# Attention operands split as whole tiles with their halves placed by DMA, the strict mask as a matmul, and the attentions' GpSimd work on other engines

## The chip, the cores and the metric

The kernel runs on one core of a Trainium2 chip. A core has five engines that run their own instruction streams: TensorE (PE, the matrix engine), VectorE (DVE), ScalarE (ACT), GpSimd (POOL) and SyncE (SP, which here only issues DMAs). They share an on-chip memory (SBUF, 128 partitions) and the matmul accumulators (PSUM, 8 banks of 128 x 512 fp32 words). The metric is the device time of one execution in microseconds (us), lower is better: the median over runs.

## What is computed

Two transformer blocks on 512 tokens of 1024 features, everything in fp32. Block 1 mixes a chunked gated linear attention (GLA) with a multi-head latent attention (MLA, 8 heads, a rotated part of 64 features beside 128 others) and has a feed-forward layer. Block 2 has two attentions of 8 heads of 64 features side by side, then a cross attention over 256 memory rows and a second feed-forward layer. The three attentions that the change touches, cut to their core:

```python
# MLA, one block of queries
s = (einsum('bqhd,bkhd->bhqk', qn_b, k_nope) + einsum('bqhr,bkr->bhqk', qp_b, k_pe)) * scale
p = softmax(where(mask, s, -inf), axis=-1)
o = einsum('bhqk,bkhd->bqhd', p, v)

# forgetting attention ("fox"), c = cumsum(log f) over the tokens
logits = einsum('bhqd,bhkd->bhqk', qi, k) * scale + ci[..., None] - c[:, :, None, :]
p = softmax(where(kpos <= qpos, logits, -inf), axis=-1)
o = einsum('bhqk,bhkd->bhqd', p, v)

# stick-breaking attention ("sb")
z = einsum('bhqd,bhkd->bhqk', qi, k) * scale
strict = kpos < qpos
log_keep = where(strict, log_sigmoid(-z), 0.0)
after = cumsum(log_keep, axis=3, reverse=True) - log_keep
a = where(strict, exp(log_sigmoid(z) + after), 0.0)
o = einsum('bhqk,bhkd->bhqd', a, v)

# block 2 around them
x = x + concat([rmsnorm(fox_o, g1), rmsnorm(sb_o, g2)]) @ w_out
x = x + memory_cross_attention(rmsnorm(x), rmsnorm(mem))
```

## The kernel before

**Numbers as pairs.** The matmuls read operands of the type fp32r; by the kernel's own note each holds 12 significant bits. Every fp32 operand is therefore split into a pair, `hi` (the value cast to fp32r) and `lo` (the value less `hi`): `hi_lo` (L129-142) makes both, `hi` on ScalarE and `lo` on VectorE unless its arguments `eh` and `el` name other engines; `pair` (L148) takes two fresh tiles for it, and `repair` (L380) frees the source as well. A product of two pairs is three matmuls, hi hi, hi lo and lo hi (`mm3`, L205-211). Heads have only 64 features, half of a tile's 128 rows, so the two attentions of block 2 and the rotated part of MLA stack the parts instead: one operand is [hi; lo] over 128 partitions (`stacked`, L1027; in MLA the tiles `Q2`, L756-761), the other a tile [hi; hi] and a tile [lo; lo] (`doubled`, L1035), and two matmuls then do the work.

In `stacked` and `doubled` each half tile of 64 rows is written by an engine of its own: casts on ScalarE and VectorE, differences on GpSimd and VectorE. For the second head of a pair `stacked` writes [lo; hi], with `hi` in the rows where the head's features stand.

**Weights.** `wload` (L175-187) loads a piece of a weight matrix by a DMA on SP's queue into one of three raw buffers (`wr`), then ScalarE casts it (`wh`, L135) and VectorE subtracts (`wl`, L139), 512 columns at a time. While `share_w` is 3 (during MLA only) every third difference goes to GpSimd.

**Order of the work.** The program is written as one Python function that emits products of layers and attention steps interleaved by hand; a scheduler that estimates times then sets the order on each engine. SBUF is cut into 84 slots of 128 x 512 words; `A` takes the slot that was freed longest ago, and whatever fills a slot waits for its last reader. Besides the slots, PSUM banks are taken in rings: for products of layers, for scores, and for sums over keys.

**The stages the change touches.** In MLA (about 325 to 450 us of the profile) `mla_pair` makes the rotated queries and the values of two heads, `mla_qk` the other queries (`qn`) and keys (`kn`), `mla_scores` and `mla_values` go head by head. In fox (950 to 1090 us) `fox_inputs` makes the operands of two heads, a pair, one pair ahead of `fox_scores`; `transposed` and `pv2_step` multiply with the values; `pv2_out` and `close` end a head. In sb (1090 to 1256 us) `sb_inputs` splits the raw queries and keys of a pair. For each of 4 key blocks `sb_keep` works out the logarithm of what the block leaves over: scores z in PSUM, three ScalarE functions into `e`, a maximum and a sum on VectorE (L1072), and the strict mask on the diagonal 128 columns by a product on GpSimd (L1073), then the pair `lkh`, `lkl` on VectorE (L1075, L1076). `sb_values` adds these in PSUM, masks the diagonal by a matmul with `nstrict_r` (L1091), exponentiates and splits the result into `ah` (GpSimd) and `al` (VectorE). Between the sb heads stand other products, from a table: the fox half of the output projection (`half_out`, L1145, its sum into x on GpSimd) and the keys and values of the memory (`memory_keys`, L971, the lower half of its pair on GpSimd). At the seam of fox and sb the norm of the fox output is worked out, with three Newton steps on VectorE (`rsqrt`, L252, on the tile `rtok`).

Of the kernel before, what the change touches and what calls it, by code (L numbers as in the profile page):

```python
# [11 lines left out]
F32R = mybir.dt.float32r  # L12
# [5 lines left out]
P = 128  # L18
# [40 lines left out]
def two_blocks(ctx: ExitStack, tc: tile.TileContext, d, dbg=None):  # L59
# [8 lines left out]
    # ------------------------------------------------------------------ helpers  # L68
    # memory is assigned in the order of the program: a slot is taken from the one freed longest ago
# [37 lines left out]
    def share(**kw):  # L107
        """which banks the products of layers, the scores and the sums over keys take in turn"""
        for name, which in kw.items():
            rings[name] = deque(which)  # L110
# [18 lines left out]
    def hi_lo(hi, lo, src, scale=None, eh=None, el=None):  # L129
        """hi + lo = scale * src, each with 12 significant bits"""  # L130
# [14 lines left out]
    # every how many parts of the weights GpSimd takes one  # L145
# [7 lines left out]
    # the tables of functions are switched here and only here: each switch waits for the functions  # L153
    # before it in the program, and the functions after it wait for the switch
# [20 lines left out]
    def wload(src):  # L175
        """(hi, lo) of each 512 columns of a part of a layer's weights"""
# [4 lines left out]
        for c in range(0, n, T):  # L181
# [3 lines left out]
            # the weights of the layer after a norm wait for the norm  # L185
# [4 lines left out]
    def wtile(w, n, kt, k0=0):  # L190
        """the weights of kt times 128 inputs for the outputs of tile n"""
        step = 8
        ws = []
        for c0 in range(0, kt, step):
            ws.append(wload(w[n, :, (k0 + c0) * P:(k0 + min(kt, c0 + step)) * P]))
        return step, ws

    def wpart(wt, k):
        """(hi, lo) of the 128 columns of input tile k"""
# [12 lines left out]
    def lin(w, n, hs, cols=T, k0=0, after=None):  # L212
        """psum[128 outputs of tile n, cols] = w[:, n].T @ h"""
# [10 lines left out]
    def lin_group(w, ns, hs, wts=None):  # L224
        """as lin for several tiles, the inputs outermost"""
# [9 lines left out]
    def lin_tok(w, b, hs, nt=NT):  # L235
        """psums[token tile][128 tokens, 512 columns of block b]"""
# [13 lines left out]
    def rsqrt(y, src, scale):  # L250
        """1/sqrt(scale * src + EPS) by Newton steps"""
# [11 lines left out]
    class Stat:  # L263
        """sum of squares over features of [features, tokens] tiles, and 1/rms of it; c: the tokens"""
# [26 lines left out]
        def done(self, c=None, direct=False):  # L291
            """1/rms of each token: along the free axis in all partitions, and [token, token tile]"""
# [24 lines left out]
    # ---------------------------------------------------------------- constants  # L317
# [42 lines left out]
    def normed(src_tiles, gain, n, before=None, **kw):  # L360
        """(hi, lo) of gain * x for each tile, and the statistics; the factor 1/rms is put on later"""
# [18 lines left out]
    def repair(x, cols=T, eh=None, el=None):  # L380
        """(hi, lo) of a tile that is freed"""
# [4 lines left out]
    # ---- where one layer ends and the next begins, the tokens go in two halves: the norms of one  # L386
    # ---- half are worked out while the products of the other run
    HALVES = (slice(0, 256), slice(256, 512))

    def last_halves(ns, wts, hs, out, after=None, stat=None, at=(0, 0)):  # L390
        """lin of the last tiles of a layer: all of them for one half of the tokens, then for the other"""
# [18 lines left out]
    def first_halves(at, ns, wts, hs, st, out, before=None, tok=None, tok_out=None):  # L410
        """lin of the first tiles of a layer, for one half of the tokens, then for the other; tok: the
        weights of a product with the tokens outermost that goes along; before: the statistics of the
        norm before; at: the steps that the sums of the norms come before, in either half."""
        for i, c in enumerate(HALVES):
# [27 lines left out]
            else:  # L442
                # the steps of this half: inputs of the product with the tokens outermost, then tiles
# [13 lines left out]
    def chained(src, gain, n, step=None):  # L457
        """(hi, lo) of gain * x for each tile, one half of the tokens after the other, and the statistics"""
# [1047 lines left out]
```

## Time and profile before

| what | value |
|---|---|
| median of 3 runs | 1779.53 us (1779.39 to 1780.85) |
| span of the profiled execution | 1780.0 us |
| PE busy | 1725.7 us, 97% |
| DVE busy | 1150.5 us, 65% |
| ACT busy | 829.5 us, 47% |
| POOL busy | 231.1 us, 13% |

The profile gives the span of the execution that it records and no other time of it. A TensorE busy share of 97% means that nearly all time is matmuls. The shares of the other engines are means over stages that differ: GpSimd does nothing in most stages and a good part of its work in the three attentions. Busy time of the matrix engine isn't all at one speed: a throttle grants it a clock, which the profile gives as a share of the full one.

### The profile page before, as it was taken

How to read it: one execution, taken by the hardware profiler on the slowest of the kernel's cores; microseconds unless marked ns; L12 is line 12 of the kernel's file. 1: busy time of each engine (PE TensorE's matmuls, PEld its weight loads, DVE VectorE, ACT ScalarE, POOL GpSimd, SP SyncE). 2: the span in 40 equal slices, each digit the busy share in tenths (PEclk: the TensorE clock that was granted, in tenths of full speed). 3: DMA queues.
4: the chain of work that ended last, by engine and by line, in shares of the span. 5: the costliest groups of instructions: out<-in, count | busy, mean ns of one | idle time of the engine just before them, and what ended most of it. 6: DMA issues, size and time to landing. Idle time of an engine off the chain costs nothing.

```text
span 1780.0 us, 24148 instructions
## 1 busy us (share of the span) xinstructions
PE 1725.7 (97%) x9007; PEld 1472.4 (83%) x9007; DVE 1150.5 (65%) x2338; ACT 829.5 (47%) x1675; POOL 231.1 (13%) x239
## 2 busy tenths in 40 slices
PE   8999999999998999999999999899999999999997
PEld 6888888888888888888887788787898988888887
DVE  7447863687749542444569667888867587547753
ACT  6534443575534332323426666566525354324442
POOL 0000000343004000000023113563310200000000
PEclk9999999999999999999999999899999999999999
DMA  6212341113531323322501121123404132432221
GB/s 222 82 48 71 93 157 36 48 54 92 181 107 51 116 78 100 109 81 84 165 10 52 54 72 60 40 74 102 136 25 134 57 107 83 131 95 83 73 82 48
DMA packets 51957, 155.30 MB, mean 87 GB/s; under 512 B 5824, under 2 KB 14720, under 8 KB 51840
## 3 DMA queue, kind: packets, MB, share of 16 engines
q1 hardware_dynamic: 51568, 153.55, 28.1%
q8 instruction: 71, 1.16, 0.3%
q14 instruction: 46, 0.38, 0.1%
q10 hardware_dynamic: 144, 0.14, 0.0%
q0 software_dynamic: 128, 0.07, 0.0%
HBM read 151.64 MB, written 2.10 MB: 86 GB/s over the span
## 4 chain that ended last, share of the span: by engine, by line
PE 83%; DVE 11%; ACT 2%; DMA 2%; issue 2%; POOL 1%; SPq 0%; DVEq 0%; ACTq 0%; POOLq 0%
PE bank L207 26%; PE bank L209 26%; PE bank L208 26%; DVE hl L141 2%; DVE wl L139 1%; DVE f L857 1%; DVE dbl L1042 1%; PE bank L734 1%; DMA wr<-w_mk 1%; DVE sq L288 1%; PE bank L300 1%; DVE dbh L1040 1%; DVE lkh L1075 1%; DMA wr<-w_mv 0%; DVE lkl L1076 0%
## 5 line engine op out<-in xcount | busy, mean ns | idle before, releaser
L139 DVE TENSOR_TENSOR wl<-wr,wh 128x512 fp32r<-128x512 f32 (+1 forms) x556 | 377.3, 694 | 289.3 <-ACT wh L135 158.9
L135 ACT CAST wh<-wr 128x512 fp32r<-128x512 f32 (+2 forms) x568 | 333.9, 608 | 458.4 <-PE bank L209 145.5
L207 PE MATMUL bank<-hh,wh 128*128 128x512 f32 (+1 forms) x1380 | 507.3, 369 | 10.2 <-ACT wh L135 7.7
L209 PE MATMUL bank<-hh,wl 128*128 128x512 f32 (+1 forms) x1380 | 506.9, 368 | 1.3 <-DVE wl L139 1.3
L208 PE MATMUL bank<-hl,wh 128*128 128x512 f32 (+1 forms) x1380 | 505.8, 367 | 0.0
L207 PEld LDWEIGHTS bank<-hh,wh 128*128 128x128 f32 x1380 | 261.9, 190 | 51.9 <-ACT wh L135 8.2
L209 PEld LDWEIGHTS bank<-hh,wl 128*128 128x128 f32 x1380 | 262.0, 190 | 44.8 <-DVE wl L139 3.6
L208 PEld LDWEIGHTS bank<-hl,wh 128*128 128x128 f32 x1380 | 262.0, 190 | 40.6 <-DVE hl L141 0.3
L208 PE MATMUL bank<-prl,wh 128*128 128x512 f32 (+1 forms) x471 | 171.4, 364 | 0.0
L209 PE MATMUL bank<-prh,wl 128*128 128x512 f32 (+1 forms) x471 | 171.4, 364 | 0.0
L207 PE MATMUL bank<-prh,wh 128*128 128x512 f32 (+1 forms) x471 | 171.2, 365 | 0.0
L207 PEld LDWEIGHTS bank<-prh,wh 128*128 128x128 f32 x471 | 88.8, 189 | 14.2
L208 PEld LDWEIGHTS bank<-prl,wh 128*128 128x128 f32 x471 | 88.9, 189 | 14.1
L209 PEld LDWEIGHTS bank<-prh,wl 128*128 128x128 f32 x471 | 88.8, 189 | 14.1
L208 PE MATMUL bank<-wl,hh 128*128 128x512 f32 (+1 forms) x192 | 71.9, 377 | 2.2 <-DVE wl L139 2.2
L858 POOL TENSOR_TENSOR x<-x,f 128x256 f32<-128x256 f32 x16 | 13.6, 848 | 459.6 <-ACT hh L137 345.8
L207 PE MATMUL bank<-wh,hh 128*128 128x512 f32 (+1 forms) x192 | 70.3, 378 | 0.1
L209 PE MATMUL bank<-wh,hl 128*128 128x512 f32 (+1 forms) x192 | 70.0, 375 | 0.3 <-DVE hl L141 0.3
L288 POOL TENSOR_TENSOR sq<-sq 128x256 f32<-128x256 f32 x56 | 46.3, 831 | 85.5 <-ACT sq L277 83.1
L137 ACT ACTIVATE hh<-x,vec 128x256 fp32r<-128x256 f32 (+1 forms) x72 | 37.7, 527 | 39.3 <-DVE x L858 16.4
L277 ACT ACTIVATE sq<-x 128x256 f32<-128x256 f32 (+1 forms) x88 | 36.7, 425 | 39.9 <-DVE x L1334 37.8
L139 POOL TENSOR_TENSOR wl<-wr,wh 128x512 fp32r<-128x512 f32 (+2 forms) x12 | 13.2, 1106 | 304.4 <-DVE wl L139 259.4
(389 smaller groups left out, 3000.7 us busy)
## 6 DMA issues: line engine op xcount, KB each, us to landing
wr<-w_fgu SPq DMA_DIRECT2D x44, 512.0 KB, 3.7
wr<-w_up SPq DMA_DIRECT2D x44, 512.0 KB, 3.7
wr<-w1T SPq DMA_DIRECT2D x16, 512.0 KB, 3.8
wr<-w_gate SPq DMA_DIRECT2D x16, 512.0 KB, 3.7
wr<-w_fd SPq DMA_DIRECT2D x16, 512.0 KB, 3.5
wr<-w2T SPq DMA_DIRECT2D x16, 512.0 KB, 3.7
wr<-w_dn SPq DMA_DIRECT2D x16, 512.0 KB, 3.6
wr<-w1K SPq DMA_DIRECT2D x12, 512.0 KB, 4.1
```

What stands on the lines that cost most here:

```text
L135: r = S.copy(hi, src) if eh is S else V.tensor_copy(hi, src)
L137: r = S.activation(hi, src, AF.Copy, scale=scale)
L139: q = el.tensor_tensor(lo, src, f(hi), ALU.subtract)
L141: q = V.scalar_tensor_tensor(lo, src, scale, f(hi), ALU.mult, ALU.subtract)
L207: r = PE.matmul(ps, lhsT=ah, rhs=bh, start=first, stop=False)
L208: PE.matmul(ps, lhsT=ah, rhs=bl, start=False, stop=False)
L209: PE.matmul(ps, lhsT=al, rhs=bh, start=False, stop=last)
L277: S.activation(q[:, :w], src, AF.Square)
L288: self.eadd.tensor_tensor(acc, acc, q[:, :w], ALU.add)
L300: i = PE.matmul(ps[:, 2 * t:2 * t + 2], lhsT=q[:, t * P:(t + 1) * P], rhs=C("ones")[:, 0:2], start=q is acc[0], stop=q is acc[-1])
L734: PE.transpose(tp[:, i * P:(i + 1) * P], ps_tiles[i][:, b * P:(b + 1) * P], C("ident"))
L857: r = V.scalar_tensor_tensor(fs[k][:, c], fs[k][:, c], vcol(gain, k), st.R[:, c], ALU.mult, ALU.mult)
```

## The change

1. *Whole-tile pairs.* The raw tile of two heads (128 rows) is split once, by `repair`: a cast on ScalarE and a difference on VectorE. `stacked` and `doubled` then only copy halves of 64 rows: `place` issues a DMA on SP's queue from one SBUF tile to another. The stacked operand is now [hi; lo] for both heads of a pair. MLA's rotated queries (`Q2`) go the same way. There are 112 such DMAs: 16 in MLA, 48 for fox and 48 for sb.
2. *Strict mask.* In `sb_keep` the product with the mask on GpSimd is gone. One more matmul of 128 columns adds `nstrict_r` (a large negative number where the key isn't strictly before the query) to z in PSUM, as `sb_values` does already. There the softplus of z becomes 0. These are 32 matmuls.
3. *GpSimd left out.* `kn` is cast on ScalarE, and its and `qn`'s differences are on VectorE. `ah` is cast on ScalarE, the lower half of the memory's keys and the sum into x are on VectorE, and `share_w` stays 0, so that VectorE makes all `wl`. In the rotation of MLA one GpSimd product per tile stays.

Outside the three attentions and what stands between their heads, each engine's order is the same. The lines of the changed program lie a little lower: `place` is L754-756, and the former L1072, L1075 and L1076 are L1074, L1076 and L1077.

```diff
...
+    def place(o, rows, src, a):
+        nc.sync.dma_start(f(o[rows]), f(src[a]))
+
+    HALF = (slice(0, 64), slice(64, 128))
+
+    def stacked(p, hh):
+        o = A("stk", F32R)
+        for rows, src in zip(HALF, p):
+            place(o, rows, src, HALF[hh])
+        return o
+
     def mla_pair(hp):
         x = evac(lin(d["w_uq"], 8 + hp, cqs), "qpe", Rq, mscale)
         rope(x)
-        Q2 = [A("Q2a", F32R), A("Q2b", F32R)]
-        S.copy(Q2[0][0:64], x[0:64])
-        G.tensor_tensor(Q2[0][64:128], x[0:64], f(Q2[0][0:64]), ALU.subtract)
-        S.copy(Q2[1][64:128], x[64:128])
-        G.tensor_tensor(Q2[1][0:64], x[64:128], f(Q2[1][64:128]), ALU.subtract)
-        free(x)
+        xp = repair(x)
+        Q2 = [stacked(xp, hh) for hh in range(2)]
+        free(xp)
...
     def mla_qk(hd):
-        qn = repair(evac(lin(d["w_uq"], hd, cqs), "qn", Rq, mscale), el=G)
-        kn = repair(evac(lin(d["w_ukvK"], hd, ckvs), "kn", Rkv), eh=V, el=G)
+        qn = repair(evac(lin(d["w_uq"], hd, cqs), "qn", Rq, mscale))
+        kn = repair(evac(lin(d["w_ukvK"], hd, ckvs), "kn", Rkv))
...
     oms = []
-    share_w[0] = 3
...
     def memory_keys(n, after=None):
-        hi_lo(mk[-1][0][:, cs], mk[-1][1][:, cs], x[:, :NMEM], el=G)
+        hi_lo(mk[-1][0][:, cs], mk[-1][1][:, cs], x[:, :NMEM])
...
-    def stacked(x, hh):
-        o = A("stk", F32R)
-        a, b = (slice(0, 64), slice(64, 128)) if hh == 0 else (slice(64, 128), slice(0, 64))
-        S.copy(o[a], x[a])
-        G.tensor_tensor(o[b], x[a], f(o[a]), ALU.subtract)
-        return o
-
-    def doubled(x, hh):
-        o1, o2 = A("dbh", F32R), A("dbl", F32R)
-        a = slice(64 * hh, 64 * hh + 64)
-        S.copy(o1[0:64], x[a])
-        V.tensor_copy(o1[64:128], x[a])
-        G.tensor_tensor(o2[0:64], x[a], f(o1[a]), ALU.subtract)
-        V.tensor_tensor(o2[64:128], x[a], f(o1[a]), ALU.subtract)
-        return o1, o2
+    def doubled(p, hh):
+        out = []
+        for src in p:
+            o = A("dbl", F32R)
+            for rows in HALF:
+                place(o, rows, src, HALF[hh])
+            out.append(o)
+        return out
...
     def sb_keep(q2, kst, b):
         PE.matmul(z[:, :w], lhsT=kst[:, dg], rhs=q2[0][:, sl], start=True, stop=False)
-        PE.matmul(z[:, :w], lhsT=kst[:, dg], rhs=q2[1][:, sl], start=False, stop=True)
+        PE.matmul(z[:, :w], lhsT=kst[:, dg], rhs=q2[1][:, sl], start=False, stop=False)
+        PE.matmul(z[:, :P], lhsT=ident_r, rhs=nstrict_r, start=False, stop=True)
...
-        G.tensor_tensor(e[:, :P], e[:, :P], C("strict"), ALU.mult)
...
     def sb_values(hd, lks, q2, kst, op, b):
-        hi_lo(ah[:, :w], al[:, :w], a[:, :w], eh=G)
+        hi_lo(ah[:, :w], al[:, :w], a[:, :w])
...
     def fox_inputs(hp):
-        out = [(stacked(xq, hh), doubled(xk, hh)) for hh in range(2)]
-        free(xq, xk)
+        pq, pk = repair(xq), repair(xk)
+        out = [(stacked(pq, hh), doubled(pk, hh)) for hh in range(2)]
+        free(pq, pk)
...
     def sb_inputs(xq, xk):
-        out = [(doubled(xq, hh), stacked(xk, hh)) for hh in range(2)]
-        free(xq, xk)
+        pq, pk = repair(xq), repair(xk)
+        out = [(doubled(pq, hh), stacked(pk, hh)) for hh in range(2)]
+        free(pq, pk)
...
     def half_out(os_, off, Ro, ns):
-            G.tensor_tensor(xs[n], xs[n], y, ALU.add)
+            V.tensor_tensor(xs[n], xs[n], y, ALU.add)
```

**Place 1, VectorE at the start of sb.** The Newton steps of the fox norm (L259 to L261, on `rtok` and the small tiles `sm`) stand among the first head's `e`, `lkh` and `lkl`. Each row is an instruction of VectorE, in its order: line, operation, output<-inputs, partitions x columns. Before:

```order
L261 SCALAR_TENSOR_TENSOR rtok_114<-sm_76,rtok_114 128x4
L1075 TENSOR_SCALAR lkh<-e 128x512
L259 TENSOR_TENSOR sm_76<-rtok_114 128x4
L1076 SCALAR_TENSOR_TENSOR lkl<-e,lkh 128x512
L1075 TENSOR_SCALAR lkh<-e 128x384
L260 TENSOR_TENSOR sm_76<-sm_76,sm_75 128x4
L1040 CAST dbh<-sq 64x512
L1076 SCALAR_TENSOR_TENSOR lkl<-e,lkh 128x384
L261 SCALAR_TENSOR_TENSOR rtok_114<-sm_76,rtok_114 128x4
L1042 TENSOR_TENSOR dbl<-sq,dbh 64x512
```

Of the change, from the same Newton step on (`mk` is the raw key tile of the memory, `mkl` the lower half of its pair):

```order
L261 SCALAR_TENSOR_TENSOR rtok_114<-sm_76,rtok_114 128x4
L139 TENSOR_TENSOR wl<-wr_74,wh 128x512
L1077 SCALAR_TENSOR_TENSOR lkl<-e,lkh 128x512
L259 TENSOR_TENSOR sm_76<-rtok_114 128x4
L375 TENSOR_TENSOR mk<-bank_66,R 128x256
L260 TENSOR_TENSOR sm_76<-sm_76,sm_75 128x4
L139 TENSOR_TENSOR wl<-wr_73,wh 128x512
L261 SCALAR_TENSOR_TENSOR rtok_114<-sm_76,rtok_114 128x4
L1074 SCALAR_TENSOR_TENSOR e<-bank_69,e 128x384
L259 TENSOR_TENSOR sm_76<-rtok_114 128x4
L139 TENSOR_TENSOR mkl<-mk,mkh 128x256
```

The pieces of the next pair's doubled tile (`dbh`, `dbl`) are gone from among the steps, and two lower halves of weights (`wl`) and the memory's keys have come between them.

**Place 2, SP's queue in sb.** The loads of the fox half of the output weights (`w_out2`) and of the memory's weights (`w_mk`, `w_mv`) into the three raw buffers `wr0` to `wr2`. Before:

```order
L179 DMA wr0_72<-w_mk 128x1024
L179 DMA wr2_74<-w_out2 128x512
L179 DMA wr2_74<-w_mk 128x1024
L179 DMA wr0_72<-w_out2 128x512
L179 DMA wr1_73<-w_mk 128x1024
L179 DMA wr0_72<-w_mk 128x1024
L179 DMA wr1_73<-w_mv 128x1024
```

Of the change, where one pair's operands are placed (`prh` and `prl` are the halves of the whole-tile pair, `x2` stands for two copies in a row into the two halves of a tile):

```order
L179 DMA wr1_73<-w_mv 128x1024
L179 DMA wr0_72<-w_mk 128x1024
L756 DMA dbl_10816<-prh_10808 64x512 x2
L756 DMA dbl_10819<-prl_10809 64x512 x2
L756 DMA stk_10822<-prh_10812 64x512
L756 DMA stk_10822<-prl_10813 64x512
L756 DMA dbl_10825<-prh_10808 64x512 x2
L756 DMA dbl_10828<-prl_10809 64x512 x2
L756 DMA stk_10831<-prh_10812 64x512
L756 DMA stk_10831<-prl_10813 64x512
L179 DMA wr2_74<-w_mv 128x1024
```

Twelve copies (four rows stand for two each) now stand in one piece between two loads of weights, and the loads behind them are issued after them.

## Rows read from the trace of the kernel before

**Rows 1.** Page, part 1: busy us, share of the span, instructions of each engine.

```profile
PE 1725.7 (97%) x9007; PEld 1472.4 (83%) x9007; DVE 1150.5 (65%) x2338; ACT 829.5 (47%) x1675; POOL 231.1 (13%) x239
```

**Rows 2.** Busy time by stretch: start:end, us, PE, PEld, DVE, ACT, POOL, PEclk, DMA, GB/s.

```profile
325.00:450.00 125.00, 122.48 (x686) 106.33 (x686) 101.40 (x266) 80.71 (x189) 50.32 (x38) 0.99 0.23 68
600.00:700.00 100.00, 100.00 (x443) 82.82 (x442) 40.69 (x64) 30.66 (x53) 0.00 (x0) 1.00 0.30 90
950.00:1090.00 140.00, 133.92 (x668) 111.12 (x667) 99.14 (x236) 88.34 (x206) 23.91 (x16) 0.98 0.18 55
1090.00:1256.00 166.00, 148.39 (x833) 129.60 (x832) 142.62 (x251) 108.49 (x232) 82.68 (x95) 0.94 0.24 72
```

**Rows 3.** Timeline, PE: start, busy us; in brackets the wait before, its releaser.

```profile
347.21 0.38 PE L208 MATMUL bank<-wl,hh 128*128 128x256 f32 x1 [2.25 <-DVE wl L139]
...
1121.34 1.12 PE L308 MATMUL bank<-con,rtok 128*128 128x128 f32 x4 [3.49 <-DVE rtok L261]
...
1139.74 0.40 PE L207 MATMUL bank<-mh,wh 128*128 128x256 f32 x1 [3.72 <-ACT wh L135]
...
1183.16 0.39 PE L209 MATMUL bank<-mh,wl 128*128 128x256 f32 x1 [3.08 <-DVE wl L139]
```

**Rows 4.** Busy time by stretch, columns as in rows 2: around the last wait.

```profile
1180.00:1190.00 10.00, 6.92 (x32) 6.27 (x32) 9.16 (x14) 4.46 (x12) 9.12 (x11) 0.72 0.19 54
```

**Rows 5.** DVE groups by form, 1088 to 1256 us: count, busy us, mean ns, idle before.

```profile
L139 DVE TENSOR_TENSOR wl<-wr,wh 128x512 fp32r<-128x512 f32 x47 | 36.1, 786 | 5.9 <-ACT wh L135 5.2 <-PE bank L1049 0.7
L1042 DVE TENSOR_TENSOR dbl<-sq,dbh 64x512 fp32r<-64x512 f32 x8 | 8.9, 1113 | 0.2
L1075 DVE TENSOR_SCALAR lkh<-e 128x512 fp32r<-128x512 f32 x8 | 6.9, 860 | 2.2 <-POOL e L1073 2.2
L1076 DVE SCALAR_TENSOR_TENSOR lkl<-e,lkh 128x384 fp32r<-128x384 f32 x8 | 6.5, 815 | 0.1
...
L1072 DVE SCALAR_TENSOR_TENSOR e<-bank,e 128x384 f32<-128x384 f32 x8 | 4.4, 553 | 2.5 <-ACT e L170 2.5
...
L1040 DVE CAST dbh<-sq 64x512 fp32r<-64x512 f32 x8 | 4.4, 545 | 0.2
```

**Rows 6.** The like with GpSimd idle: DVE timeline at 1117, groups 600 to 900 us.

```profile
1117.40 0.43 DVE L1075 TENSOR_SCALAR lkh<-e 128x512 fp32r<-128x512 f32 x1
...
L139 DVE TENSOR_TENSOR wl<-wr,wh 128x512 fp32r<-128x512 f32 x99 | 67.2, 690 | 106.3 <-PE bank L208 52.9 <-ACT wh L135 49.6 <-ACT z L170 1.6
```

**Rows 7.** ACT groups by form, 1088 to 1256 us.

```profile
L135 ACT CAST wh<-wr 128x512 fp32r<-128x512 f32 x49 | 29.7, 618 | 29.4 <-DMA wr<-w_mk 6.0 <-DVE lkl L1076 5.5 <-DVE bol L141 3.5
```

**Rows 8.** POOL groups by form, 1088 to 1256 us.

```profile
L1073 POOL TENSOR_TENSOR e<-e,con 128x128 f32<-128x128 f32 x32 | 18.4, 584 | 21.7 <-DVE e L1072 19.4 <-DVE sm L260 1.9
```

**Rows 9.** Timeline, PE, at 1135 us: two matmuls of 128 columns in a row.

```profile
1135.19 0.28 PE L1091 MATMUL bank<-nstrict_r,ident_r 128*128 128x128 f32 x1
1135.31 0.27 PE L1085 MATMUL bank<-dbh,stk 128*128 128x128 f32 x1
```

**Rows 10.** DVE groups by form, 950 to 1090 us.

```profile
L1042 DVE TENSOR_TENSOR dbl<-fk,dbh 64x512 fp32r<-64x512 f32 x6 | 7.4, 1238 | 0.2
```

**Rows 11.** DVE groups by form, 325 to 450 us.

```profile
L139 DVE TENSOR_TENSOR wl<-wr,wh 128x512 fp32r<-128x512 f32 x14 | 11.6, 839 | 1.4 <-ACT wh L135 0.7 <-PE bank L734 0.4 <-PE bank L208 0.3
...
L135 DVE CAST prh<-kn 128x512 fp32r<-128x512 f32 x8 | 6.1, 767 | 0.1
```

**Rows 12.** Timeline, SP, issuing loads; then DMA issues, us to landing.

```profile
2.15 1.39 SPq L325 DMA_DIRECT2D x<-xT  x3
...
wr<-w2T SPq DMA_DIRECT2D x16, 512.0 KB, 3.7
...
wr<-w_out SPq DMA_DIRECT2D x16, 256.0 KB, 2.8
...
wr<-w_ukvK SPq DMA_DIRECT2D x8, 128.0 KB, 2.0
```

## The prediction, made before the changed kernel was run

> **What bounds the kernel now.** I read the page's busy shares first: TensorE (PE) is busy for 1725.7 of 1780.0 us, GpSimd (POOL) for 231.1 [rows 1]. With PE at 97% the most that a rearrangement can win is what PE waits, 54 us, and what it computes at a lowered clock. So the second view is the busy time by stage [rows 2]: the three attentions that the change touches are MLA (325 to 450 us), the forgetting attention "fox" (950 to 1090) and the stick-breaking attention "sb" (1090 to 1256). PE waits 125 - 122.5 = 2.5 us in the first, 140 - 133.9 = 6.1 in the second and 166 - 148.4 = 17.6 in the third, 26.2 together. The same rows give the granted clock, 0.99, 0.98 and 0.94: (1 - clock) x length is 1.3 + 2.8 + 10.0 = 14.1 us of lost clock. The third view says why: the clock falls after PE has stood still. From 1180 to 1190 us PE waits 3.1 us and the granted clock is 0.72 [rows 3, 4], that is, a part of the stretch ran at the lower of its two levels (1.2 instead of 2.4 GHz). A stall is so paid for almost one and a half times. Together 40 us can be won, and no more.
>
> Who is waited for: the timeline names VectorE (DVE) behind the long waits (the lower half of a weight, `wl`; the Newton steps of a norm, `rtok`) and ScalarE's weight cast `wh` behind one [rows 3]. In sb DVE is busy for 142.6 of 166 us, in the stage 600 to 700, where PE never waits, for 41 of 100 [rows 2]. So the third stage is one where DVE is nearly as full as PE.
>
> A part of DVE's time is no work. In sb the same instruction is long or short: `lkh` of 128x512 takes 860 ns in the mean [rows 5], one that ran with GpSimd idle took 430 [rows 6]; `wl` takes 786 against 690 in the stage without GpSimd; `lkl` of 128x384 takes 815, and `e` of the same size, which reads one operand from PSUM, 553. DVE instructions on SBUF operands stretch where GpSimd works beside them, and GpSimd works for half of the sb stage, 82.7 us [rows 2].
>
> **The change part by part, sb.** *Taken off DVE:* the doubled tiles' differences `dbl` (8.9 us) and casts `dbh` (4.4) [rows 5], 13.3 us. *Put on DVE:* the differences of 8 whole tiles (sq and sk of four pairs, 8 x 0.69 = 5.5), 8 additions to x (8 x 0.69 = 5.5, from `wl`'s unhindered row, also two SBUF operands of 128x512 [rows 6]) and 8 halves of the memory's keys, 128x256 (8 x 0.42 = 3.4, an estimate by 0.69 x 256/512 and the fixed part that 553 against 690 shows), 14.4. *Given back by an idle GpSimd:* 47 x (786 - 690) = 4.5, 8 x (860 - 430) = 3.4, 8 x (815 - 553) = 2.1, so 10.0 from three rows [rows 5, 6]; the 80 other pieces of `lkh`, `lkl` and `al` I take at 0.11 each, a third of what the last two rows give per piece: 9. In sum -13.3 + 14.4 - 19 = -18, DVE goes from 142.6 to about 125 us. ScalarE loses 16 half-tile casts and gets 8 whole ones at the same 0.618 [rows 7] (-4.9) and 32 casts `ah` of 128 to 512 columns, by their mean width 32 x 0.43 = 13.9: from 108.5 to 117.5, still under DVE. The GpSimd step between `e` and `lkh`, 0.58 us each [rows 8], leaves the chain of each key block, and 32 matmuls of 128 columns take its place, 0.12 us from one start to the next [rows 9]: +3.8 us on PE, which is the bound, so they count in full.
>
> What that is worth: PE's own work in sb at full clock is 148.4 - 10.0 + 3.8 = 142 us, DVE's 125, 88% of it; MLA runs today with DVE busy for 101.4 of 125 us, 81%, and PE waits there 2% with the clock at 0.99. Were sb as good, it would take 142/0.97 = 146.5 us, 19.5 less than 166. I take a bit over half, **-11**, because not all of its waits hang on DVE's length: 3.7 us are behind ScalarE's weight cast [rows 3], and ScalarE gets more to do. Bounds: -19.5, and +4 if no wait goes.
>
> *The Newton steps.* The largest single wait that I count on is `rtok`'s 3.49 us at 1121 [rows 3]: between the steps DVE's order held pieces of the next pair's doubled tiles, which are gone there; now a weight's difference and the memory's keys stand between them, but the whole chain begins earlier against PE's matmuls. I count no loss.
>
> **Fox.** DVE loses 8 `dbl` at 1.24 [rows 10] = 9.9 and 8 casts at 0.545 [rows 5] = 4.4, and gets 8 x 0.69 = 5.5: -8.8 of 99.1. The waits to win are 6.1 and 2.8 us of clock, mostly between 968 and 990. Half: **-4.4** (bounds 0 and -8.9).
>
> **MLA.** DVE gets 20 differences of whole tiles (qn, kn, the rotated part: 13.8) and the 12 weight parts that GpSimd took (6 of 0.69, 6 of about 0.5: 7.1), and loses 8 casts of kn at 0.767 = 6.1 and its stretching, 14 x (839 - 690) = 2.1 for `wl` [rows 11] and, by the same ratio for the softmax scaling and the rope sum, some 7: +5 of 101.4, to 87% of PE's time. That cover is thin: **+1**, with bounds -3.8 (all of 2.5 and 1.3 won) and +13 (sb's present share of waits, 10.6%, at nearly the same DVE load).
>
> **The DMAs.** 112 copies of 64 rows x 512 (128 KB): 4 for each of 4 MLA pairs, 12 for each of 4 + 4 pairs later, all on SP's queue, where all weight loads are issued. No copy within SBUF stands in the trace. Issue: three in 1.39 us, 0.46 each [rows 12], so 12 hold the queue for 5.6 us. Landing: 2.0 us by the 128 KB load, 2.8 by the 256 KB one [rows 12]; I take 2.8, since a copy both reads and writes SBUF. A copy waits in the queue for the cast or difference that it copies and for the last reader of the slot that it fills, and the weight loads behind it wait too; who waits for those is ScalarE's `wh`, DVE's `wl` and then PE. The cover of a burst is the weights already split: one tile is 24 matmuls of 0.226 us (443 in the 100 us of the full stage [rows 2]), 5.4 us, about the 5.6 of the burst. Most pairs are copied a head or two ahead, which hides the landing. One is not: the first sb pair, where the lower half of q goes to a slot that the last `fo` step frees; from there 0.5 + 2.8 = 3.3 us stand against 2 us of PE's work, 1.3 exposed. With one more such spot for the weights, **+3**; bounds 0 and the rival below.
>
> Sum against the profiled execution: 1780.0 - 11 - 4.4 + 1 + 3 = 1768.6. The page gives only its span; the runs' median is 1779.53, 0.5 less, so **1768 us**.
>
> **Rivals.** *The queue (slower).* If a copy of 64 rows moves at half the rate of 128 rows, each costs what 256 KB cost: 0.9 us more for each further 256 KB (2.8 to 3.7 [rows 12]), a burst 12 x 0.9 = 10.8 us, 5.4 more than the cover. A wait of that size also draws the lower clock. At one landing and half a slow stretch, 3.7 + 1.7, in half of the eight bursts that is 21.6 us, against 14.4 won: 1779.5 + 7 = **1787**. It decides from 14.4/8 = 1.8 us a burst. For it: 20 copies stand in a row in places, and each sits ahead of the loads. Against: DMA is busy for 18 to 24% of these stages [rows 2]. The Trainium skill says this outright: "DMA: Bandwidth & Descriptors", Rules for kernel authors, advises against two transfers to disjoint halves of the partitions, since they serialize, and for one of 128 partitions; "SBUF — State Buffer", Door 1, has 64 partitions reach 8 of 16 ports. By these the burst would cost the 10.8 us; no row of this trace shows a copy within SBUF.
>
> *Nothing (same).* PE's order is fixed; if the waits are chains and not DVE's load, they form anew a matmul later, and the 3.8 us of PE stay against a few us won: **1779**. For it: `wh` is as often waited for as `wl`. Against: the stretching is measured.
>
> *All of it.* Waits in the three stages sink to what 600 to 700 us shows: 19.5 + 8.9 + 3.8 = 32: **1747**. Against: DVE at 88%.
>
> **How the numbers follow.** Forecast (1758 to 1775) 0.54, everything won 0.12, nothing 0.13, queue 0.21. Faster 0.66, same 0.13, slower 0.21, by the 0.2% (3.6 us) that a measurement of this kernel can tell from no change. The range leaves out the better half of the second case and the upper third of the last: 1750 to 1789.
>
> **What would show it.** Right: in sb `lkh` of 512 columns near 430 ns and `wl` near 690, DVE near 125 us, PE's waits halved and fewer stretches under a clock of 1; 32 more matmuls at L1069. Wrong: PE waiting for `wh` behind a weight DMA that SP issued after a burst; copies landing in over 4 us; new waits in MLA with DVE at 90%.

## The result and the profile after

The changed kernel takes 1769.47 us (median, 1765.36 to 1772.74) against 1779.46 before on the same chip. The ratio is 0.9938, with a 95% interval from 0.9922 to 0.9955. That is 11 us by the ratio and 10 by the medians, inside the range, and 1.5 us above the predicted 1768. The profile of after spans 1767.9 us. That execution's time was 1769.93 us, and in the executions below the time is 1.7 to 2.2 us above the span. The profile of before, 1780.0, so belongs to an execution of about 1782: of the 12.1 us between the two profiles some 2 are scatter.

The page's busy shares after, to be set against [rows 1]:

```profile
PE 1724.3 (98%) x9039; PEld 1472.6 (83%) x9039; DVE 1111.8 (63%) x2366; ACT 832.1 (47%) x1695; POOL 71.7 (4%) x87
```

PE has 32 matmuls more and is busy 1.4 us less, since less of it runs at the lower clock. VectorE lost 39 us, GpSimd 159. The same three stretches as in [rows 2] (us, busy time of PE, PEld, DVE, ACT, POOL, then the granted clock, DMA share, GB/s):

```profile
325.00:450.00 125.00, 123.73 (x699) 106.81 (x699) 104.60 (x291) 84.06 (x192) 7.23 (x4) 1.00 0.30 87
950.00:1090.00 140.00, 136.26 (x686) 112.64 (x685) 87.05 (x230) 85.70 (x201) 0.00 (x0) 1.00 0.40 106
1090.00:1256.00 166.00, 155.18 (x911) 136.16 (x909) 123.51 (x275) 115.76 (x259) 0.00 (x0) 0.98 0.44 124
```

PE waits 1.3, 3.7 and 10.8 us, where it waited 2.5, 6.1 and 17.6. These stretches are fixed times, and the changed kernel is some 8 us further on in the last of them. VectorE in sb has 123.5 us, in the prediction about 125. The pieces of VectorE that stretched beside GpSimd, in sb (groups by form: count, busy us, mean ns, idle before):

```profile
L139 DVE TENSOR_TENSOR wl<-wr,wh 128x512 fp32r<-128x512 f32 x53 | 35.3, 685 | 14.4 <-ACT wh L135 13.8 <-ACT ah L135 0.4
...
L1077 DVE SCALAR_TENSOR_TENSOR lkl<-e,lkh 128x384 fp32r<-128x384 f32 x8 | 4.4, 550 | 0.0
...
L1076 DVE TENSOR_SCALAR lkh<-e 128x512 fp32r<-128x512 f32 x8 | 3.4, 421 | 0.0
```

They took 786, 815 and 860 ns [rows 5]. The predicted values were 690, 553 and 430.

What PE still waits for, around sb (the waits by what released them: total us, times, longest):

```profile
PE bank L1050 <- DVE so L1058: 4.6, 3, 2.4
PE bank L207 <- ACT R L314: 3.8, 1, 3.8
PE bank L207 <- DVE sm L260: 2.0, 1, 2.0
```

The first is a chain that the prediction didn't name: sb has one PSUM bank for the sums over keys, and the next head's first `pv2_step` waits until the last head's sum is copied out (`pv2_out`, L1058). The second is the seam to the next layer, the third the seam from fox to sb, told below. The longest wait that the prediction counted on, 3.49 us for `rtok`, is gone.

**Stages.** For a comparison over all kernels each stage is cut at the first matmul of a norm's sum (L300 of the changed kernel). In the timeline of after:

```profile
324.47 0.72 PE L300 MATMUL bank<-con,sq 128*128 128x2 f32 x6
...
528.30 0.61 PE L300 MATMUL bank<-con,sq 128*128 128x2 f32 x4 [0.93 <-DVE sq L288]
...
942.68 0.50 PE L300 MATMUL bank<-con,sq 128*128 128x2 f32 x4
...
1104.51 0.72 PE L300 MATMUL bank<-con,sq 128*128 128x2 f32 x6
...
1290.56 0.51 PE L300 MATMUL bank<-con,sq 128*128 128x2 f32 x4
```

"MLA" is the first two of them (with the gates and the mix behind MLA), "fox" the third to the fourth, "sb" the fourth to the fifth. One profile each, in us; ratios come from the timed rounds:

| kernel | MLA | fox | DVE in fox | sb | DVE in sb | fox + sb | ratio to before (95%) |
|---|---|---|---|---|---|---|---|
| before | 205.9 | 169.0 | 125.8 | 190.4 | 161.0 | 359.4 | 1 |
| after | 203.8 | 161.8 | 103.3 | 186.1 | 141.3 | 347.9 | 0.9938 (0.9922 to 0.9955) |
| strict mask alone | 206.3 | 171.0 | 129.0 | 184.1 | 150.0 | 355.1 | 0.9966 (0.9954 to 0.9978) |
| after without DMAs | 206.1 | 171.0 | 128.1 | 182.9 | 148.3 | 353.9 | 0.9980 (0.9971 to 0.9990) |
| placement alone | 213.6 | 160.7 | 104.4 | 182.6 | 150.0 | 343.3 | 0.9973 (0.9961 to 0.9984) |
| placement in fox and sb alone | 205.2 | 160.0 | 104.5 | 185.4 | 149.8 | 345.4 | 0.9933 (0.9915 to 0.9951) |
| after, mask on GpSimd | 205.8 | 163.3 | 104.5 | 183.4 | 145.8 | 346.6 | 0.9933 (0.9918 to 0.9948) |
| after, MLA as before | 206.1 | 161.8 | 103.3 | 182.8 | 142.4 | 344.7 | 0.9930 (0.9913 to 0.9946) |

The scatter is to be read from stages whose code is the same: after and "MLA as before" share sb and differ there by 3.2 us. A profile is also one execution: that of the strict mask alone is 3.3 us above the median of its runs, that of the placement alone 2.4 below.

The cut between fox and sb is not at the same place in TensorE's work. In the first two kernels, by the groups of the fox stage:

```profile
L207 PE MATMUL bank<-mh,wh 128*128 128x256 f32 x8 | 2.3, 292 | 1.0 <-DVE sk L375 1.0
```

```profile
L207 PE MATMUL bank<-mh,wh 128*128 128x256 f32 x4 | 1.2, 308 | 0.4 <-ACT wh L135 0.4
```

In the five kernels of the table that place by DMA, 12 products of the memory's keys and two of the first sb scores stand behind the cut instead of ahead of it: about 1.8 us, an estimate by their starts (12 x 0.12 and 2 x 0.17). So 1.8 of what these kernels win in "fox" is work that moved to "sb". The column "fox + sb" is free of it.

### The profile page after: what moved, and what is told of

Same layout as the page of the kernel before. It is cut to its first block, busy times and chain, and to the rows that moved or that the text cites. A ratio compares the mean times of both kernels' runs of the same rounds, so it can differ in the third digit from the quotient of the medians.

```text
span 1767.9 us, 24298 instructions
## 1 busy us (share of the span) xinstructions
PE 1724.3 (98%) x9039; PEld 1472.6 (83%) x9039; DVE 1111.8 (63%) x2366; ACT 832.1 (47%) x1695; POOL 71.7 (4%) x87
## 3 DMA queue, kind: packets, MB, share of 16 engines
q1 hardware_dynamic: 60528, 168.24, 31.8%
## 4 chain that ended last, share of the span: by engine, by line
PE 88%; DVE 6%; ACT 3%; DMA 2%; issue 1%; SPq 0%; DVEq 0%; ACTq 0%
PE bank L207 27%; PE bank L209 27%; PE bank L208 27%; DVE wl L139 1%; PE bank L1091 1%; DVE f L866 1%; PE bank L734 1%; DVE hl L141 1%; ACT wh L135 1%; DMA wr<-w_mq 1%; DMA wr<-w_out 0%; DMA wr<-w_o_gla 0%; PE bank L300 0%; PE bank L1050 0%; PE bank L1051 0%
## 5 line engine op out<-in xcount | busy, mean ns | idle before, releaser
L139 DVE TENSOR_TENSOR wl<-wr,wh 128x512 fp32r<-128x512 f32 (+2 forms) x568 | 375.3, 676 | 310.0 <-ACT wh L135 180.1
L288 POOL TENSOR_TENSOR sq<-sq 128x256 f32<-128x256 f32 x56 | 46.6, 836 | 410.8 <-ACT sq L277 408.4
L141 DVE SCALAR_TENSOR_TENSOR hl<-x,vec,hh 128x256 fp32r<-128x256 f32 (+1 forms) x72 | 46.2, 659 | 3.7 <-ACT hh L137 3.7
L375 DVE TENSOR_TENSOR z<-bank,R 128x512 f32<-128x512 f32 x38 | 26.1, 686 | 33.4 <-PE bank L209 33.4
```

The costliest lines, as they stand in the source:

```text
L139: q = el.tensor_tensor(lo, src, f(hi), ALU.subtract)
L141: q = V.scalar_tensor_tensor(lo, src, scale, f(hi), ALU.mult, ALU.subtract)
L288: self.eadd.tensor_tensor(acc, acc, q[:, :w], ALU.add)
L375: V.tensor_tensor(o[:, :cols], ps[:, :cols], Rt[:, :cols], ALU.mult)
```

## The experiments

### The parts, one at a time

**The strict mask alone.** Before, with `sb_keep` of the change:

```diff
-        PE.matmul(z[:, :w], lhsT=kst[:, dg], rhs=q2[1][:, sl], start=False, stop=True)
+        PE.matmul(z[:, :w], lhsT=kst[:, dg], rhs=q2[1][:, sl], start=False, stop=False)
+        PE.matmul(z[:, :P], lhsT=ident_r, rhs=nstrict_r, start=False, stop=True)
...
-        G.tensor_tensor(e[:, :P], e[:, :P], C("strict"), ALU.mult)
```

> The kernel before with the strict mask by matmul alone. Theory (VectorE's load decides): 32 matmuls cost 3.8 us of TensorE, 18.4 us less of GpSimd give VectorE back some 4 us, so within 3 us of before, 1777 to 1782. Rival (the chain of the strict mask counted): 32 x 0.58 us shorter chains show, about 1771.

Measured: 1773.94 us (1771.15 to 1777.26), ratio 0.9966, 6 us less. That misses the theory's range on the fast side and comes near the rival. In the stages sb alone is shorter, by 6.3 us (fox is 2.0 longer). Its busy times there, before and then with the mask by matmul:

```profile
1112.30:1302.71 190.41, 171.91 (x1036) 153.25 (x1036) 161.03 (x302) 113.88 (x250) 86.53 (x104) 0.95 0.27 82
```

```profile
1114.01:1298.12 184.11, 170.66 (x1064) 153.63 (x1063) 149.96 (x299) 112.85 (x247) 69.11 (x74) 0.97 0.27 85
```

`lkh` of 512 columns fell from 860 to 557 ns and `lkl` of 384 from 815 to 701. VectorE's 11.1 us less in this stage are not all relief: three of its instructions (two `wl`, one `mk`) have moved ahead of the cut, and it has 3.2 us more in fox. Over the whole kernel, by the page, GpSimd lost 19.3 us and VectorE 7.5, more than the "some 4" expected:

```profile
PE 1726.9 (97%) x9039; PEld 1474.4 (83%) x9039; DVE 1143.0 (64%) x2338; ACT 830.2 (47%) x1675; POOL 211.8 (12%) x207
```

So a microsecond of GpSimd beside VectorE cost 0.4 of VectorE here. The chain from `e` to `lkh` became shorter too (from the end of the one to the start of the other 1.65 us in the mean of 32 blocks before, 0.69 here), and this run alone doesn't tell the two apart.

**The changed kernel with the mask back on GpSimd.** The same lines turned round, on the changed kernel.

> The changed kernel with the strict mask back on GpSimd and without the 32 matmuls. Theory (VectorE's load decides): 3.8 us less of TensorE against 18.4 us of GpSimd beside VectorE, near the changed kernel, 1766 to 1771. Rival (the chain of the strict mask counted): 1775 to 1778.

Measured: 1767.78 us (1767.0 to 1769.62), ratio 0.9933: no different from the changed kernel. The chain is longer again (1.19 us in the mean against 0.57) and costs nothing, so the chain isn't what decides, at least with the rest of the change. Nor do 32 matmuls fewer show in the time; PE is busy 2.8 us less (1721.5 against 1724.3). The page:

```profile
PE 1721.5 (97%) x9007; PEld 1467.5 (83%) x9007; DVE 1116.1 (63%) x2366; ACT 832.3 (47%) x1695; POOL 90.9 (5%) x119
```

GpSimd has 19.2 us more than in the changed kernel and VectorE only 4.3, for the same 2366 instructions: 0.2 us for each.

**The changed kernel without its DMAs.** `stacked` and `doubled` of the kernel before, with VectorE in GpSimd's place:

```diff
     def doubled(x, hh):
         o1, o2 = A("dbh", F32R), A("dbl", F32R)
         a = slice(64 * hh, 64 * hh + 64)
         S.copy(o1[0:64], x[a])
         V.tensor_copy(o1[64:128], x[a])
-        G.tensor_tensor(o2[0:64], x[a], f(o1[a]), ALU.subtract)
+        V.tensor_tensor(o2[0:64], x[a], f(o1[a]), ALU.subtract)
         V.tensor_tensor(o2[64:128], x[a], f(o1[a]), ALU.subtract)
```

> The changed kernel without its DMAs: halves are cast and subtracted by engines as before, but on VectorE where GpSimd did it, so GpSimd stays out and the mask is a matmul. VectorE gets about 3.7 us more for each pair, 14.7 in fox and in sb each. Theory (VectorE's load decides): most of the gain in fox and sb goes, 1776 to 1780. Rival (GpSimd's absence is the gain, the DMAs cost 3): 1766.

Measured: 1776.4 us (1774.52 to 1780.89), ratio 0.9980, as the theory had it; the rival (1766) falls. The stages say more than the total. Fox, cut from norm to norm, before, without the DMAs and after:

```profile
943.34:1112.30 168.96, 160.75 (x809) 132.57 (x808) 125.75 (x293) 108.37 (x249) 39.47 (x26) 0.98 0.20 60
```

```profile
943.08:1114.08 171.00, 162.47 (x814) 134.98 (x812) 128.11 (x317) 110.30 (x249) 0.00 (x0) 0.97 0.20 59
```

```profile
942.68:1104.51 161.83, 157.64 (x798) 129.47 (x797) 103.27 (x274) 99.92 (x233) 0.00 (x0) 1.00 0.44 115
```

Without GpSimd but with VectorE as loaded as before (128 us), fox stays at 171. With 103 us it takes 162, and the clock rises to 1.00. So it is the placement that shortens fox. By VectorE's load alone it is not shown: ScalarE's goes the same way (108.4, 110.3 and 99.9 us in the three rows), and no run relieves only one of the two. In sb, however, the kernel without DMAs is as short as any (182.9), with VectorE at 148.

**Placement alone.** The kernel before with `repair`, `place` and the new `stacked` and `doubled` everywhere, MLA included; everything else stays on GpSimd.

> The kernel before with the first part of the change alone: whole-tile pairs and 112 placing DMAs; GpSimd keeps the strict mask, ah, the memory's keys, the sums into x and its part of MLA. Theory (VectorE's load decides): VectorE loses 8 to 9 us in fox, some 12 in sb, GpSimd about 25 us of halves; a good half of the gain comes back, about 1774 us. Rival (the gain is GpSimd's absence, the DMAs only cost): 1780 to 1787. Rival (the chain of the strict mask is what counted): 1779.

Measured: 1775.85 us (1773.47 to 1777.42), ratio 0.9973, near the theory's number, but not in its way: fox and sb together won 16.0 us in the profile and MLA lost 7.7. In MLA, PE waits there:

```profile
412.50 0.50 PE L207 MATMUL bank<-hh,wh 128*128 128x512 f32 x1 [0.79 <-ACT wh L135]
414.53 0.80 PE L209 MATMUL bank<-hh,wl 128*128 128x512 f32 x1 [1.30 <-POOL wl L139]
```

and ScalarE's casts before the first of these came late, one waiting for its load and the next, which PE waited for, close behind it:

```profile
410.97 0.62 ACT L135 CAST wh<-wr 128x512 fp32r<-128x512 f32 x1 [2.13 <-DMA wr<-w_gate]
411.82 0.62 ACT L135 CAST wh<-wr 128x512 fp32r<-128x512 f32 x1 [0.24 <-DMA stk<-prh]
```

SP issued that load at 404.8 us and four copies behind it until 408.4. It landed some 6 us after its issue, where the gate's weights take 3.7 in the median before. The next weight's difference is one that GpSimd still makes. The two waits are 2.1 of the 7.6 us that PE waits in MLA here. Which of them, or what else, makes MLA slow here, and not in the changed kernel, was not tried and stays open.

**Placement in fox and sb alone.** The same, with MLA's code as before.

```diff
+    def place(o, rows, src, a):
+        nc.sync.dma_start(f(o[rows]), f(src[a]))
...
     def fox_inputs(hp):
+        pq, pk = repair(xq), repair(xk)
+        out = [(stacked(pq, hh), doubled(pk, hh)) for hh in range(2)]
...
     def sb_inputs(xq, xk):
+        pq, pk = repair(xq), repair(xk)
+        out = [(doubled(pq, hh), stacked(pk, hh)) for hh in range(2)]
```

> The kernel before with the whole-tile pairs and placing DMAs in fox and sb alone (96 copies); MLA, the strict mask, ah, the memory's keys and the sums into x as before, on GpSimd. Theory (in fox and sb the placement alone brings the whole gain, the other parts relieve the same VectorE again and bring nothing on top): as the changed kernel, 1766 to 1770. Rival (the gains of the parts add: 4 us by the placement, 6 by the mask, the rest by the others): about 1775.

Measured: 1767.12 us (1766.16 to 1770.47), ratio 0.9933. The theory holds: this part alone gives what the whole change gives, with GpSimd still busy for 75 us of sb (86.5 before):

```profile
941.68:1101.67 159.99, 156.75 (x795) 129.24 (x794) 104.45 (x278) 101.39 (x238) 1.01 (x2) 1.00 0.44 117
1101.67:1287.05 185.38, 170.40 (x1049) 150.74 (x1048) 149.83 (x301) 111.22 (x246) 75.20 (x97) 0.98 0.37 108
```

**The changed kernel with MLA as before.**

```diff
-        qn = repair(evac(lin(d["w_uq"], hd, cqs), "qn", Rq, mscale))
-        kn = repair(evac(lin(d["w_ukvK"], hd, ckvs), "kn", Rkv))
+        qn = repair(evac(lin(d["w_uq"], hd, cqs), "qn", Rq, mscale), el=G)
+        kn = repair(evac(lin(d["w_ukvK"], hd, ckvs), "kn", Rkv), eh=V, el=G)
...
+    share_w[0] = 3
```

and `mla_pair` of the kernel before.

> The changed kernel with MLA as before (GpSimd's differences and every third weight difference, no DMAs there). Theory (MLA won 2 us by the change, more than was forecast): 1771 to 1772. Rival (MLA was a gain of nothing and the difference is spread): 1769. As the prediction had it (+1): 1768.

Measured: 1768.75 us (1767.29 to 1769.25), ratio 0.9930. MLA's part of the change is worth nothing that shows: its code before took 205.2 to 206.3 us in five kernels, that of the change 203.8 to 209.0 in five.

### What the copies cost

The copies after, by what they fill (count, KB each, median us from issue to landing):

```profile
dbl<-prh SPq DMA_DIRECT2D x32, 128.0 KB, 2.8
dbl<-prl SPq DMA_DIRECT2D x32, 128.0 KB, 2.5
...
stk<-prh SPq DMA_DIRECT2D x24, 128.0 KB, 2.6
stk<-prl SPq DMA_DIRECT2D x24, 128.0 KB, 2.4
```

and SP's queue at the start of sb:

```profile
1087.69 1.11 SPq L756 DMA_DIRECT2D dbl<-prh  x2
1088.85 0.59 SPq L756 DMA_DIRECT2D stk<-prh  x1
...
1104.29 0.60 SPq L756 DMA_DIRECT2D stk<-prl  x1
1104.94 1.13 SPq L179 DMA_DIRECT2D wr<-w_out  x2
```

In these 18 us the 16 DMA engines are busy for 83% of the time (the last share but one), where the stretch from 1090 to 1256 us has 0.44:

```profile
1087.00:1105.00 18.00, 17.55 (x98) 14.61 (x96) 13.06 (x25) 12.02 (x26) 0.00 (x0) 1.00 0.83 191
```

Two pairs, 24 copies, hold the queue for 17 us, and the load behind them lands late: ScalarE waits 2.3 us for it, VectorE 1.6 us for ScalarE, and PE 2.0 us for VectorE.

```profile
1108.52 0.62 ACT L135 CAST wh<-wr 128x512 fp32r<-128x512 f32 x1 [2.32 <-DMA wr<-w_out]
```

```profile
1109.17 0.69 DVE L139 TENSOR_TENSOR wl<-wr,wh 128x512 fp32r<-128x512 f32 x1 [1.57 <-ACT wh L135]
...
1110.46 0.41 DVE L375 TENSOR_TENSOR mk<-bank,R 128x256 f32<-128x256 f32 x1
```

```profile
1111.02 0.77 PE L207 MATMUL bank<-boh,wh 128*128 128x512 f32 x1 [2.00 <-DVE sm L260]
```

The Newton step that the profile names (`sm`, L260) ended last, but the product has no use for it. In VectorE's order the late `wl` stands ahead of the copying out of `mk`, which ends at 1110.87; most likely the product waits for the PSUM bank that this frees.

**Each copy twice.**

```diff
-        nc.sync.dma_start(f(o[rows]), f(src[a]))
+        for _ in range(2):
+            nc.sync.dma_start(f(o[rows]), f(src[a]))
```

> The changed kernel with each placing DMA issued twice, 112 more copies of the same halves. At 0.6 us of SP's queue each, a burst of 12 grows by 7 us. Theory (a burst mostly hidden, about 0.4 us exposed of each now): three of the eight bursts show, 1776 to 1784. Rival (the queue is the limit): 8 x 7, over 1800. Rival (hidden): 1769 to 1772.

Measured: 1794.64 us (1793.47 to 1795.1), ratio 1.0077, so 25 us over the changed kernel by the ratios: dearer than the theory's 7 to 15, cheaper than the rival's 56. It cost MLA 9 us, fox 14 and sb 2, and now PE itself waits for copies (in fox and sb):

```profile
PE bank L1111 <- DMA dbl<-prl: 3.7, 2, 2.8
```

The run costs more than 112 further issues, however. The second copy writes what the first has just written, and SP now waits for copies to land, 30 us in all between 940 and 1200 us, where it waits for none in the changed kernel. The longest of these groups:

```profile
SPq L757 <- DMA dbl<-prl: 13.0, 23, 2.7
```

So the bursts have no cover left for this, but how much of the 25 us is the number of copies and how much the waiting of one for the other is not shown. That the first 112 cost as much does not follow; "MLA as before" takes 16 of them away and wins nothing.

**The copies on GpSimd's queue.**

```diff
-        nc.sync.dma_start(f(o[rows]), f(src[a]))
+        nc.gpsimd.dma_start(f(o[rows]), f(src[a]))
```

> The changed kernel with the 112 placing DMAs issued from GpSimd's queue instead of SP's, so that no weight load stands behind them. Theory (the copies' place ahead of the weight loads costs about 3 us, first of all the 2.0 us wait at the start of sb): 1764 to 1767. Rival (issuing from GpSimd costs VectorE as GpSimd's work did, or lands late): 1772 or more.

Measured: 1772.16 us (1771.03 to 1773.94), ratio 0.9953 (0.9938 to 0.9967): the theory's gain is not there, and the run is at the rival's lower end. Against the changed kernel (0.9938) it is not clear of the scatter. VectorE isn't stretched (`lkh` of 512 columns 421 ns, as after), but the copies land later, 3.2 to 3.8 us instead of 2.4 to 2.8:

```profile
dbl<-prh POOLq DMA_DIRECT2D x32, 128.0 KB, 3.2
dbl<-prl POOLq DMA_DIRECT2D x32, 128.0 KB, 3.8
```

None of PE's waits in fox and sb names a copy in this run, so that the later landing costs time is not shown.

**The weight loads among the copies.** The next sb pair's operands are written behind the products between the heads.

```diff
-        if hd % 2 == 0 and hd < 6:
-            sin_.append(sb_inputs(*sraw[hd // 2 + 1]))
         last = (hd, lks, q2, kst, o)
         between(fill[hd])
+        if hd % 2 == 0 and hd < 6:
+            sin_.append(sb_inputs(*sraw[hd // 2 + 1]))
```

> The changed kernel with the operands of the next sb pair written behind the products between the heads instead of ahead of them; SP's order then has weight loads among the copies at the start of sb, where 24 copies stood in a row. Theory (the burst ahead of the loads costs 2 to 3 us): 1765 to 1768. Rival (hidden anyway): 1769.

Measured: 1768.32 us (1766.46 to 1770.93), ratio 0.9931 against 0.9938: within the scatter. The loads of `w_out2` were issued from 1097 us on, among the copies, and the wait changed its name:

```profile
1108.46 0.73 PE L207 MATMUL bank<-boh,wh 128*128 128x512 f32 x2 [1.49 <-ACT boh L137]
```

The product now waits 1.5 us for its other operand, the last fox head under its gain (`boh`). But the wait for the weights has not gone, it has moved 4 us ahead: ScalarE, which makes `boh` as well, waits as long for a load of `w_out2` as before, and `boh` comes behind that cast.

```profile
1104.33 0.62 ACT L135 CAST wh<-wr 128x512 fp32r<-128x512 f32 x1 [2.27 <-DMA wr<-w_out]
```

So this run doesn't show what the seam costs without that wait.

**The same edit on the kernel with the placement in fox and sb alone**, tried as a version that might beat both.

> The kernel before with the placement in fox and sb alone, and the operands of the next sb pair written behind the products between the heads. Theory (what is left of the placement's cost is the 24 copies in a row ahead of the weight loads at the start of sb, a wait of 2.2 us there with a stretch of lower clock): 1 to 3 us less than with the placement in fox and sb alone, 1764 to 1766. Rival (the next wait, for the norm's Newton steps on VectorE, ends there anyway): 1767.

Measured: 1769.01 us (1767.47 to 1769.51), ratio 0.9933 (0.9919 to 0.9947): the rival again. No kernel of this study is measurably faster than the changed one.

### What is left in sb

**Two banks for the sums over keys**, the second taken from the products of layers or from the scores:

```diff
-    share(mm=(0, 1, 2), at=(3, 4, 5, 6), op=(7,))
+    share(mm=(0, 1), at=(3, 4, 5, 6), op=(2, 7))
```

```diff
-    share(mm=(0, 1, 2), at=(3, 4, 5, 6), op=(7,))
+    share(mm=(0, 1, 2), at=(3, 4, 5), op=(6, 7))
```

> The changed kernel with two PSUM banks instead of one for the sums over keys in sb, the second taken from the products of layers (two instead of three). Theory (what is left of the waits in sb are other chains, first of all the single bank: 4.6 us of waits for the last head's sum to be copied out): 3 to 5 us less than the changed kernel, 1765. Rival (VectorE's load decides still, the wait comes back elsewhere): 1769. With fewer banks for products it could also lose.

> As the run with two banks for the sums over keys, but with the second taken from the scores (three instead of four). Theory (the single bank's 4.6 us): 1765. Rival (the waits come back elsewhere): 1769; a ring of three for the scores may cost as much.

Measured: 1771.44 us (1768.37 to 1776.59), ratio 0.9955, and 1769.85 us (1767.89 to 1770.74), ratio 0.9941. The rivals: the 4.6 us of waits for the single bank are gone from both profiles, and other waits have come; in the first one above all for the Newton steps:

```profile
1107.17 1.11 PE L308 MATMUL bank<-con,rtok 128*128 128x128 f32 x4 [3.58 <-DVE rtok L261]
```

Both edits also move the order of the work, so they don't price the bank by itself. They show that taking away the largest group of waits that is left does not shorten the kernel.

## Why the prediction was right, and where it was not

The time came out as forecast: the sum was 1768.6 against a span of 1767.9. Its steps did not all hold.

- **GpSimd stretches VectorE.** Right, to about 2% in the three rows that it priced, and VectorE's 123.5 us in sb is the forecast 125. What a microsecond of GpSimd costs VectorE is no constant: the mask's step cost it 7.5 us in the kernel before and 4.3 in the changed one, where less of GpSimd's other work runs beside it.
- **sb, -11 with the DMAs' +3.** The profiles give -4.4 for the changed kernel and -7.6 for the same sb code with MLA as before; for the same work some 1.8 more, -6 and -9, against a net -8. The size is right, the step that leads to it is not. It took PE's waits as a function of VectorE's load and went "a bit over half" the way for 18 us of relief. The table shows rather a step: VectorE from 161 to 150 us (mask alone, placement alone, or no GpSimd with the old halves) makes sb 5 to 8 us shorter, and from 150 to 141 nothing more that the scatter of 3 us lets see. Kernels with different parts of the change each win this gain, and all parts together win it once. The waits that are left name other chains: the single bank, the seams' norms, the first weights behind the copies.
- **Fox, -4.4.** About right: -7.1 in the changed kernel by the cut, some -5.3 for the same work, and by the same account -4 to -7 in the seven profiles with single copies on SP's queue and the sums in one bank. Only the placement does it (160 to 165 us with, 169 to 171 without). What the prediction took for half of 8.9 us of waits and lost clock was a little more: from 950 to 1090 us the clock went from 0.98 to 1.00 and PE's waits from 6.1 to 3.7 us. VectorE lost 12.1 us in that stretch, not 8.8. The prediction put it all down to VectorE; ScalarE's relief, some 8 us, goes along and was not tried by itself.
- **MLA, +1.** The profile says -2.1, the run with MLA as before says nothing that shows. Within the bounds, but the edit is idle there, and with GpSimd's part kept it was a loss of 7.7 us.
- **32 matmuls, +3.8.** PE's busy time says 2.8 (against the mask on GpSimd), the clock's share in it unknown. In the time it doesn't show.
- **The DMAs, +3.** Landing 2.4 to 2.8 us was the 2.8 taken; issuing took 0.6 us of SP's queue each, not 0.46. Twelve copies so took 8.6 us of the queue at the start of sb, not 5.6. The longest exposed spot is the one foretold, the first sb pairs, but through the weights behind the copies (2.0 us): none of PE's waits there names a copy.
- **The queue, the slower rival.** It did not come. It rested on 3.7 us for a copy and 5.4 us beyond the cover for each burst. The DMA queue's share of the span is 28.1% of 1780.0 us before and 31.8% of 1767.9 after, which is 62 us of all 16 engines for 112 copies, 0.55 us each, a little less than the 0.6 that SP needs to issue one. In a burst both are nearly full, the 16 engines for 83% of the time from 1087 to 1105 us. With each copy twice there is a loss, 25 us, as the rival has it, but part of it is the waiting of a copy for the one before. The Trainium skill ("DMA: Bandwidth & Descriptors", Rules for kernel authors) advises against transfers to disjoint halves of the partitions because they serialize; no run here moved whole tiles in place of halves, so the rule stays untested, but its price, as the prediction worked it out, was not met.
- **The rival "nothing"** named the true limit of the forecast: waits do form anew elsewhere (two banks, loads first). It came one step of relief too early.

So the likeliest case came true, and by its main terms: fox and sb with the DMAs were forecast at -12.4 us together and measured -11.5 in the changed kernel, -14.7 with MLA as before. MLA came out 3 us cheaper than forecast in the one profile, and the stages that the change doesn't touch 1.5 us longer; both are within the scatter, and that the sum fits to 1 us is luck.

## What to carry to other kernels

Where an engine that feeds TensorE is at 85% of a stage and in step with it, its load may pay down to some point only, here about 150 of 185 us by single profiles: of several edits that relieve the same engine, try each alone, for the cheapest may give all of it. Splitting a tile once and placing its halves by DMA took 21 us of VectorE's 126 out of the fox stage for 72 copies (48 for fox, 24 for the first two sb pairs) of 0.6 us each on a queue that had room. Before adding copies, look at which loads stand behind them on that queue: with each copy issued twice the whole gain and 14 us more were gone.

## What the runs showed of the hardware

- A copy of 64 rows x 512 words from SBUF to SBUF lands 2.4 to 2.8 us after its issue on SP's queue and 3.2 to 3.8 us on GpSimd's. Issuing takes 0.6 us on SP and 0.52 on GpSimd.
- GpSimd work on SBUF tiles lengthened VectorE's: the mask's 19 us on GpSimd cost VectorE 7.5 us in the kernel before and 4.3 in the changed one. Not only instructions with two SBUF inputs were stretched: `lkh`, with one, took twice its time. The Trainium skill ("SBUF — State Buffer", SBUF: two separate sides) has the two engines lock a pair of ports against each other, which the loser waits out in full. The trace agrees in that an instruction of 0.42 us took 0.86 in the mean and ScalarE's casts of 128x512 take 618 ns [rows 7] in both kernels.
- The DMA instructions that GpSimd issued (0.52 us each, 96 in fox and sb) did not visibly stretch VectorE: `lkh` stayed at 421 ns.
